# A two-block language-model forward pass on one Trainium2 core: expert down weights in 8 KB runs, shorter fillers at the router's gates, a fixed TensorE order behind them, and a reordered start

## The chip, the core and the metric

The kernel runs on one core of a Trainium2 chip. A core has five engines that each take their own instructions in order and meet through semaphores: TensorE (PE in the profile; its weight loads are listed as PEld) does matrix products into PSUM, VectorE (DVE) and ScalarE (ACT) do elementwise work and empty PSUM, GpSimd (POOL) is almost unused here, and SyncE (SP) issues nearly all transfers. Transfers run on 16 DMA engines that all queues share. The metric is the device time of one execution in microseconds (us); lower is better. All numbers are float32; products of activations with weights are made from high and low halves in a rounded type (fp32r), three products for one.

## The reference, cut to what matters

The input is 256 tokens and 16 meta tokens of width 1024. A first block has two layers, each a mixer (a short convolution, then latent attention) and a mixture of 64 experts; a second block of two layers follows, which the change leaves alone. The experts take most of the time and all of the weight traffic that the change touches.

```python
def hier_moe(hn, w_grp, w_exp, w_gate, w_up, w_down):
    g_logits = xf @ w_grp                     # 8 groups
    grp = argmax(g_logits); p_g = max(softmax(g_logits))
    e_in = (xf @ w_exp).reshape(n, 8, 8)[grp] # the 8 experts of that group
    top_p, top_i = top_k(softmax(e_in), 2)
    gate = p_g * top_p / sum(top_p)
    ...                                       # tokens sorted by expert
    def expert_block(xb, e):
        hh = silu(xb @ w_gate[e]) * (xb @ w_up[e])   # 1024 -> 256
        return hh @ w_down[e]                        # 256 -> 1024
    ...                                       # added back, weighted by gate

h = h + short_conv_mixer(rmsnorm(h), w_in, conv_w, w_out)   # layer 0
h = h + hier_moe(rmsnorm(h), ...)                           # layer 0
h = h + mla_mixer(rmsnorm(h), ...)                          # layer 1
h = h + hier_moe(rmsnorm(h), ...)                           # layer 1
return second_block(rmsnorm(h))                             # two more layers
```

## The kernel before

One Python program records all instructions, and a scheduler then sets the order on each engine. Inside `in_order(engine)` the instructions of that engine are chained as they are written; with `after=True` the chain is also tied to the last instruction before it. Elsewhere the scheduler may put one instruction between others.

**Weights.** `make_plan` (L161) lists every weight transfer of 1 MB in the order of use; SP issues them. `ahead` keeps `depth` of them under way, and 20 buffers (`WBUFS`) hold them with other tiles; a transfer waits until its buffer is free. `wload` (L119) puts row k*128+p of a matrix on partition p; `wload_flat` (L126) gives each partition one run of memory. For each expert, gate and up (1024 x 256) go by `wload_flat`: partition p gets 8 rows, 8 KB in one run. Down (256 x 1024) goes by `wload`: partition p gets rows p and 128+p, two runs of 4 KB.

**Start.** `start` (L438) issues constants and the tokens (three tiles `x` of 16, 128 and 128 rows) on SP and a few vectors on ACT's queue. The router's table `rt` (w_grp in runs of 32 bytes, w_exp in runs of 256 bytes) is written in `router` (L592, L593) on ACT's queue, and the scheduler put it early. `enter_tokens` (L507) runs ten unread products of a zero tile, turns the vectors, and transposes the tokens in eight column tiles k of three transposes each. For each k, ACT makes the high half `hnh`, DVE the low half `hn`, and ACT or DVE in turn copies the raw tile to `hT`. Then `split` makes high and low halves `wh` (ACT) and `wl` (DVE, in two pieces) of each convolution weight, and `dense` multiplies.

**Gates.** `router` sums the squares of each token by products with a column of ones; DVE copies them to `ssum` (L636). `choose` (L679) takes, on DVE, the best group, the best two experts and their one-hot rows `asg`. On TensorE it writes `keep_busy` (L673), transposes of the identity that nobody reads (48 in layer 0, 40 in layer 1), then products that count `asg` into places, then 24 more unread transposes. DVE makes `cm` from the counts and the selection `sel` from `cm`; the three low halves `hp` of the last token columns stand before `cm` on DVE. `weigh` (L734) then makes the weights of the chosen experts.

**Experts.** 16 quads of four experts each. `enter` (L842) gathers the tokens of the first two quads with `sel` (products `pa`), ACT scales them to `xg`, and the first gate products `pg` follow in four steps; the first quad's gate weights come in four transfers, each holding 2 of the 8 columns k for all four experts. `slots4` (L963) turns `sel` for one quad (`pt`), which ACT copies to `selT`. `gate_up`, then `down` (L873): two transposes of `sg`, products `pd` with the down weights, and products `pc` that add the rows back.

Of the kernel before, what the change touches and what calls it, by code (L numbers as in the profile page):

```python
# [20 lines left out]
D = 1024  # L21
KT = 8
S = 256
META = 16
T = META + S
# [3 lines left out]
CAP = 32  # L29
# [81 lines left out]
class Builder:  # L111
# [49 lines left out]
    def make_plan(self):  # L161
        a, P = self.a, []
# [8 lines left out]
        def moe(layer, following):  # L171
            for q in range(NE // 4):
# [12 lines left out]
                for e in range(4 * q, 4 * q + 4):  # L185
                    s = a["w_down"][layer, e]
                    P.append(lambda s=s: self.wload(s, 2, D))

# [22 lines left out]
        for l in range(2):  # L211
# [8 lines left out]
            for half in range(2):  # L220
                for g in range(4):
                    s = a["w_out_2"][l, 1024 * half:1024 * half + 1024]
# [284 lines left out]
    def enter_tokens(self, vectors):  # L507
# [5 lines left out]
        with self.in_order(nc.tensor):  # L513
            p = self.bank("tp")
            for i in range(10):
                self.mm(p[:, 128 * (i % 4):128 * (i % 4) + 128], zero[:, :128], zero[:, :128], True, True)
            vectors()
            for k in range(KT):
                p = self.bank()
                for (t0, n), x in zip(TILES, self.xs):  # L520
                    nc.tensor.transpose(p[:, t0:t0 + n], x[:, 128 * k:128 * k + 128], self.ident[:n, :n])
                col = g[:, k:k + 1]
                nc.scalar.activation(out=hi[:, k], in_=p[:, :T], func=AF.Identity, scale=col)
                V.scalar_tensor_tensor(lo[:, k], p[:, :T], col, hi[:, k].bitcast(F32), op0=ALU.mult, op1=ALU.subtract)
                self.copy(self.hT[:, k], p[:, :T], "va"[k % 2])
        return hi, lo
# [54 lines left out]
    def router(self, layer, new, lgt, tpt):  # L581
# [9 lines left out]
        rt = self.cp.tile([128, KT, 72], F32, name="rt", tag="rt")  # L591
        nc.scalar.dma_start(out=rt[:, :, 0:8], in_=a["w_grp"][layer].rearrange("(k p) e -> p k e", p=128))  # L592
        nc.scalar.dma_start(out=rt[:, :, 8:72], in_=a["w_exp"][layer].rearrange("(k p) e -> p k e", p=128))  # L593
        with self.in_order(V, after=True):
# [40 lines left out]
        for i, (t0, n) in enumerate(self.tiles):  # L635
            V.tensor_copy(self.ssum[:n, i:i + 1], ps[:n, i:i + 1])  # L636
        yield
# [41 lines left out]
    def choose(self, mp, tl):  # L679
# [36 lines left out]
        V.tensor_add(asg, oh2[:, :, 0], oh2[:, :, 1])  # L716
        self.keep_busy(48 - 8 * self.layer)
        pc = self.bank()
# [11 lines left out]
        self.cm = cm  # L730
        self.keep_busy(24)
        return oh2, asg, cm, L, gm, em, self.select(mp, 0)
# [140 lines left out]
    def down(self, mp, sg, selT, gcol, take, nE, by_expert=False):  # L873
# [4 lines left out]
        for c in range(2):  # L878
            nc.tensor.transpose(pt[:, M * c:M * c + M], sg[:M, 128 * c:128 * c + 128], self.ident[:M, :M])
        st = mp.tile([128, 2, 128], F32, name="st", tag="st", bufs=2)  # L880
# [6 lines left out]
        for h, c, e in order:  # L887
            self.mm(pd[h][CAP * e:CAP * e + CAP], st[:, c, CAP * e:CAP * e + CAP], ws[e][:, c, 512 * h:512 * h + 512],
                    c == 0, c == 1)
# [11 lines left out]
    def moe(self, layer):  # L901
# [5 lines left out]
        with tc.tile_pool(name="mo", bufs=1) as mp:  # L907
            NQ = NE // 4
            four = lambda: [self.take() for _ in range(4)]
            with ExitStack() as st:  # L910
                with tc.tile_pool(name="rt", bufs=1) as rp:
# [4 lines left out]
                    self.depth = DEPTH["experts"]  # L916
                    with self.in_order(nc.tensor, after=True):
                        xg, pg = self.enter(sel, four)
                    with self.in_order(V, after=True):
                        code, counts = weigh()  # L920
                mq = st.enter_context(tc.tile_pool(name="me", bufs=1))
                with self.in_order(nc.scalar, V, after=True):
                    to = self.slots4(mq, sel, 0)
                for q in range(NQ):
                    last = q == NQ - 1
# [52 lines left out]
    def overflown(self, mp, layer, code, over):  # L978
# [6 lines left out]
        with tc.If(n > 0), tc.For_i(0, n, 1) as it:  # L985
# [13 lines left out]
            gu = lambda: [self.wload_flat(a[next(names)][layer, ds(e, 1)].rearrange("o (p k) m -> p (o k m)", p=128))]  # L999
            dn = lambda: [self.wload(a["w_down"][layer, ds(e, 1)].rearrange("o f d -> (o f) d"), 2, D)]  # L1000

# [811 lines left out]
```

## Time and profile before

| | |
|---|---|
| time, median of 3 runs | 1880.17 us (1880.01 to 1880.68) |
| profiled execution, its own time | 1876.76 us |
| span of the profiled execution, first to last instruction | 1874.5 us |
| TensorE busy | 1630.6 us (87%) |
| DVE / ACT busy | 899.4 us (48%) / 622.7 us (33%) |
| HBM read | 523.20 MB, 280 GB/s over the span |
| chain that ended last, by engine | PE 53%, DMA 37%, DVE 5%, ACT 3% |
| of it, DMA into `w` from w_up / w_down / w_gate | 17% / 13% / 7% |
| of it, unread transposes (L677) | 1% |

The share of busy time is a mean over stages with different limits, so the stages are read one by one: from the chain of waits in order of time which resource ends last, from the tables by stretch how busy the transfers are and at which clock TensorE runs (1.00 is 2.4 GHz, 0.50 is 1.2 GHz), and from the timeline which instruction an engine stood waiting for (in square brackets behind a row: idle time and what ended it). The convolution fills the first 132 us, the gates and experts of layer 0 run to about 620 us, latent attention to 742 us, the gates and experts of layer 1 to about 1220 us, and the second block the rest.

### The profile page before, as it was taken

How to read it: one execution, taken by the hardware profiler on the slowest of the kernel's cores; microseconds unless marked ns; L12 is line 12 of the kernel's file. 1: busy time of each engine (PE TensorE's matmuls, PEld its weight loads, DVE VectorE, ACT ScalarE, POOL GpSimd, SP SyncE). 2: the span in 40 equal slices, each digit the busy share in tenths (PEclk: the TensorE clock that was granted, in tenths of full speed). 3: DMA queues.
4: the chain of work that ended last, by engine and by line, in shares of the span. 5: the costliest groups of instructions: out<-in, count | busy, mean ns of one | idle time of the engine just before them, and what ended most of it. 6: DMA issues, size and time to landing. Idle time of an engine off the chain costs nothing.

```text
span 1874.5 us, 32357 instructions
## 1 busy us (share of the span) xinstructions
PE 1630.6 (87%) x13515; PEld 1226.6 (65%) x13515; DVE 899.4 (48%) x2065; ACT 622.7 (33%) x1194; POOL 1.2 (0%) x6
## 2 busy tenths in 40 slices
PE   8999878787877999877767777799999999999997
PEld 7986444443443778543433333389999998999997
DVE  6753322211213675231221222288786647888673
ACT  5422011100120552210110011065456747545673
POOL 0000000000000000000000000000000000000000
PEclk8999989889988999999989898999999999999999
DMA  9667999999999337799999999944373425337340
GB/s 305 198 253 312 415 418 415 418 415 418 416 408 397 121 135 292 315 416 418 416 417 416 416 417 408 404 154 135 114 224 113 135 90 163 113 114 224 113 136 23
DMA packets 192095, 526.39 MB, mean 281 GB/s; under 512 B 15927, under 2 KB 115642, under 8 KB 160202
## 3 DMA queue, kind: packets, MB, share of 16 engines
q1 hardware_dynamic: 187644, 523.65, 73.5%
q8 instruction: 108, 1.77, 0.4%
q10 hardware_dynamic: 4302, 0.63, 0.2%
q14 instruction: 41, 0.34, 0.1%
HBM read 523.20 MB, written 1.05 MB: 280 GB/s over the span
## 4 chain that ended last, share of the span: by engine, by line
PE 53%; DMA 37%; DVE 5%; ACT 3%; issue 1%; SPq 0%; DVEq 0%; ACTq 0%
PE mm L244 30%; DMA w<-in_w_up_dram 17%; DMA w<-in_w_down_dram 13%; DMA w<-in_w_gate_dram 7%; PE A L244 5%; PE pg L244 4%; PE O L244 3%; PE pa L244 3%; PE pd L244 3%; PE pc L244 1%; PE idle L677 1%; DVE hT L505 1%; DVE wl L273 1%; PE T L244 1%; PE pt L244 1%
## 5 line engine op out<-in xcount | busy, mean ns | idle before, releaser
L244 PE MATMUL pg<-w,xg 128*32 128x256 f32 x4096 | 354.2, 433 | 116.2 <-DMA w<-in_w_gate_dram 85.0
L244 PEld LDWEIGHTS pg<-w,xg 128*32 128x32 f32 x4096 | 154.7, 123 | 278.2 <-DMA w<-in_w_gate_dram 118.4
L273 DVE TENSOR_TENSOR wl<-w,wh 128x1024 fp32r<-128x1024 f32 x192 | 231.1, 1218 | 37.9 <-ACT wh L258 29.2
L505 DVE TENSOR_TENSOR hT<-hT,pc 128x272 f32<-128x272 f32 (+1 forms) x256 | 99.7, 426 | 287.3 <-PE pc L244 287.0
L244 PE MATMUL mm<-xnh,wh 128*128 128x256 f32 x768 | 223.0, 291 | 2.7 <-ACT xnh L258 1.4
L244 PE MATMUL mm<-xnh,wl 128*128 128x256 f32 x768 | 218.0, 284 | 4.3 <-DVE wl L273 4.3
L244 PE MATMUL mm<-xn,wh 128*128 128x256 f32 x768 | 219.4, 286 | 1.8 <-DVE xn L1318 1.0
L244 PE MATMUL pd<-w,st 128*32 128x512 f32 x1024 | 183.7, 612 | 23.9 <-DVE st L239 15.5
L258 ACT ACTIVATE wh<-w 128x2048 fp32r<-128x2048 f32 x96 | 182.5, 1907 | 38.6 <-PE mm L244 24.0
L244 PEld LDWEIGHTS mm<-xnh,wl 128*128 128x128 f32 x768 | 147.6, 192 | 5.4 <-DVE wl L273 4.9
L244 PEld LDWEIGHTS mm<-xnh,wh 128*128 128x128 f32 x768 | 147.4, 192 | 5.4 <-ACT xnh L258 1.9
L244 PEld LDWEIGHTS mm<-xn,wh 128*128 128x128 f32 x768 | 147.6, 192 | 4.1 <-DVE xn L1318 1.4
L237 ACT ACTIVATE selT<-pt 128x272 fp32r<-128x272 f32 (+1 forms) x32 | 12.5, 391 | 408.9 <-PE pt L244 270.4
L894 DVE SCALAR_TENSOR_TENSOR o<-pd,gcol,o 128x512 fp32r<-128x512 f32 x64 | 48.1, 751 | 205.2 <-ACT o L893 196.9
L244 PEld LDWEIGHTS pd<-w,st 128*32 128x32 f32 x1024 | 48.0, 111 | 123.3 <-issue 75.9
L244 PE MATMUL pc<-selT,o 128*128 128x272 f32 (+1 forms) x512 | 106.8, 329 | 22.9 <-DVE hT L505 21.9
L244 PEld LDWEIGHTS pc<-selT,o 128*128 128x128 f32 x512 | 76.2, 198 | 70.3 <-issue 36.8
L893 ACT ACTIVATE o<-pd,gcol 128x512 fp32r<-128x512 f32 x64 | 44.0, 687 | 221.7 <-PE pd L244 172.7
L244 PE MATMUL pa<-sel,hp 128*128 128x256 f32 x640 | 83.6, 287 | 0.2
L244 PEld LDWEIGHTS pa<-sel,hp 128*128 128x128 f32 x640 | 78.4, 190 | 5.4 <-ACT xg L237 2.9
L870 DVE TENSOR_TENSOR sg<-sg,pg 128x256 f32<-128x256 f32 x32 | 13.5, 421 | 99.5 <-ACT sg L869 99.5
L244 PE MATMUL mm<-hnh,wh 128*128 128x272 f32 x192 | 57.1, 298 | 0.1
(531 smaller groups left out, 2867.3 us busy)
## 6 DMA issues: line engine op xcount, KB each, us to landing
w<-in_w_gate_dram SPq DMA_DIRECT2D x128, 1024.0 KB, 19.2
w<-in_w_up_dram SPq DMA_DIRECT2D x128, 1024.0 KB, 19.9
w<-in_w_down_dram SPq DMA_DIRECT2D x128, 1024.0 KB, 20.1
w<-in_w_in_dram SPq DMA_DIRECT2D x60, 1024.0 KB, 5.3
w<-in_w_out_dram SPq DMA_DIRECT2D x16, 1024.0 KB, 5.0
w<-in_conv_w_in_dram SPq DMA_DIRECT2D x12, 1024.0 KB, 13.0
w<-in_conv_w_out_dram SPq DMA_DIRECT2D x4, 1024.0 KB, 5.3
w<-in_w_o_dram SPq DMA_DIRECT2D x4, 1024.0 KB, 5.4
```

The source lines that it names most:

```text
L237: self.nc.scalar.activation(out=out, in_=in_, func=f, scale=scale)
L244: self.nc.tensor.matmul(out, lhsT, rhs, start=start, stop=stop)
L258: nc.scalar.activation(out=hi, in_=x, func=AF.Copy)
L273: V.tensor_tensor(out=lo[:, k], in0=x[:, k], in1=h[:, k], op=ALU.subtract)
L505: self.nc.vector.tensor_add(self.hT[:, k, t0:], self.hT[:, k, t0:], ps)
L677: self.nc.tensor.transpose(p[:, 128 * (i % 4):128 * (i % 4) + 128], self.ident, self.ident)
L870: nc.vector.tensor_tensor(out=sg[:M], in0=sg[:M], in1=pg[:M, 256:], op=ALU.mult)
L893: nc.scalar.activation(out=oh[:M, d], in_=pd[h][:M], func=AF.Identity, scale=gcol[:M])
L894: nc.vector.scalar_tensor_tensor(ol[:M, d], pd[h][:M], gcol[:M], oh[:M, d].bitcast(F32), op0=ALU.mult, op1=ALU.subtract)
```

## The change

Six edits.

1. Down weights go by `wload_flat`: partition p gets rows 2p and 2p+1, one run of 8 KB. So that the products meet the right rows, `down` transposes columns c, c+2, c+4, ... of `sg` (`sg[:M, c::2]`) in place of a block of 128, and reads the weights at 1024c. The loop for overflowing experts is changed alike.
2. The unread transposes at the gates fall from 48 (layer 0) and 40 (layer 1) to 26, and from 24 to 10 behind the counts.
3. TensorE's chain at the gates stays open through `enter`, `weigh` and the first `slots4`.
4. `ssum` is copied by ACT, no longer by DVE.
5. Layer 0's table `rt` is issued on SP. Layer 1's stays on ACT's queue.
6. `enter_tokens` runs 12 unread products in place of 10, gives each of the eight column tiles its own PSUM bank from the start, and copies to `hT` only behind the first weight's split.

```diff
-                    s = a["w_down"][layer, e]
-                    P.append(lambda s=s: self.wload(s, 2, D))
+                    s = a["w_down"][layer, e].rearrange("(p c) d -> p (c d)", p=128)
+                    P.append(lambda s=s: self.wload_flat(s))
...
-            p = self.bank("tp")
-            for i in range(10):
+            p = self.bank("lg")
+            for i in range(12):
...
-            for k in range(KT):
-                p = self.bank()
+            banks = [self.bank(t) for t in ("mm",) * 4 + ("tp",) * 2 + ("lg", "mm")]
+            for k, p in enumerate(banks):
...
-                self.copy(self.hT[:, k], p[:, :T], "va"[k % 2])
+        self.presplit(1)
+        for k, p in enumerate(banks):
+            self.copy(self.hT[:, k], p[:, :T], "va"[k % 2])
...
-        nc.scalar.dma_start(out=rt[:, :, 0:8], in_=a["w_grp"][layer].rearrange("(k p) e -> p k e", p=128))
-        nc.scalar.dma_start(out=rt[:, :, 8:72], in_=a["w_exp"][layer].rearrange("(k p) e -> p k e", p=128))
+        queue = nc.scalar if layer else nc.sync
+        queue.dma_start(out=rt[:, :, 0:8], in_=a["w_grp"][layer].rearrange("(k p) e -> p k e", p=128))
+        queue.dma_start(out=rt[:, :, 8:72], in_=a["w_exp"][layer].rearrange("(k p) e -> p k e", p=128))
...
-            V.tensor_copy(self.ssum[:n, i:i + 1], ps[:n, i:i + 1])
+            self.copy(self.ssum[:n, i:i + 1], ps[:n, i:i + 1], "a")
...
-        self.keep_busy(48 - 8 * self.layer)
+        self.keep_busy(26)
...
-        self.keep_busy(24)
+        self.keep_busy(10)
...
-            nc.tensor.transpose(pt[:, M * c:M * c + M], sg[:M, 128 * c:128 * c + 128], self.ident[:M, :M])
+            nc.tensor.transpose(pt[:, M * c:M * c + M], sg[:M, c::2], self.ident[:M, :M])
...
-                    with self.in_order(nc.tensor, after=True):
-                        xg, pg = self.enter(sel, four)
+                    turn = st.enter_context(ExitStack())
+                    turn.enter_context(self.in_order(nc.tensor, after=True))
+                    xg, pg = self.enter(sel, four)
...
                     to = self.slots4(mq, sel, 0)
+                turn.close()
```

TensorE at the gates of layer 1, before; `pa` gathers tokens, `pc` counts experts, `pt` turns the selection, `pg` is the first gate product:

```order
L677 MATMUL idle<-const_64 128x128 x24
L244 MATMUL pa<-sel,hp 128x256 x16
L244 LDWEIGHTS ones_462
L244 MATMUL pc<-asg,ones_462 128x64
L244 LDWEIGHTS ones_462
L244 MATMUL pc<-asg,ones_462 128x64
L957 MATMUL pt<-const_64,sel 128x128 x2
L244 MATMUL pt<-g_6550,sel 128x5 x2
L957 MATMUL pt<-const_64,sel 128x128 x2
L244 MATMUL pt<-g_6550,sel 128x5 x2
L244 MATMUL pg<-w,xg 32x256 x8
L244 MATMUL pa<-sel,hp 128x256 x8
```

And now, at the same place:

```order
L680 MATMUL idle<-const_64 128x128 x10
L244 MATMUL pa<-sel,hp 128x256 x16
L244 MATMUL pg<-w,xg 32x256 x8
L244 MATMUL pa<-sel,hp 128x256 x8
L244 MATMUL pg<-w,xg 32x256 x8
L244 MATMUL pa<-sel,hp 128x256 x8
L244 MATMUL pg<-w,xg 32x256 x16
L244 LDWEIGHTS ones_464
L244 MATMUL pc<-asg,ones_464 128x64
L244 LDWEIGHTS ones_464
L244 MATMUL pc<-asg,ones_464 128x64
L962 MATMUL pt<-const_64,sel 128x128 x2
```

The counting and turning products moved from between the gather and the first gate product to behind all four steps of `enter`; in layer 0 they stood there already. ACT's copies follow: the two `selT` of layer 1 stood ahead of the eight `xg` and now stand behind them.

ACT at the start, before:

```order
L396 ACT_TABLE_LOAD
L592 DMA rt<-in_w_grp_dram 128x8x8
L593 DMA rt<-in_w_exp_dram 128x8x64
L523 ACTIVATE hnh<-mm,vec_67 128x272 x6
L237 ACTIVATE hT<-mm 128x272
L258 ACTIVATE wh<-w 128x2048
L237 ACTIVATE hT<-mm 128x272
L523 ACTIVATE hnh<-mm,vec_67 128x272
L237 ACTIVATE hT<-mm 128x272
L523 ACTIVATE hnh<-mm,vec_67 128x272
L258 ACTIVATE wh<-w 128x2048
```

And now:

```order
L396 ACT_TABLE_LOAD
L523 ACTIVATE hnh<-mm,vec_67 128x272 x4
L523 ACTIVATE hnh<-tp,vec_67 128x272 x2
L523 ACTIVATE hnh<-lg,vec_67 128x272
L523 ACTIVATE hnh<-mm,vec_67 128x272
L258 ACTIVATE wh<-w 128x2048
L237 ACTIVATE hT<-mm 128x272 x2
L237 ACTIVATE hT<-tp 128x272
L237 ACTIVATE hT<-mm 128x272
L258 ACTIVATE wh<-w 128x2048
```

The table's two transfers left the queue, and the first weight's high half moved from behind six `hnh` to behind all eight.

SP in the convolution, now; `raw` are small vectors of the second block:

```order
L435 DMA const_462<-in_const_dram 128x1725
L123 DMA w<-in_conv_w_in_dram 128x8x256
L474 DMA raw<-in_pre_norm_dram 16x128
L474 DMA raw<-in_post_norm_dram 16x128
L474 DMA raw<-in_hgrn_lb_logits_dram 16x128
L474 DMA raw<-in_hgrn_out_norm_dram 2x128
L474 DMA raw<-in_cmp_b_k_dram 2x128
L123 DMA w<-in_conv_w_in_dram 128x8x256 x3
L474 DMA raw<-in_cmp_b_v_dram 2x128
L595 DMA rt<-in_w_grp_dram 128x8x8
L596 DMA rt<-in_w_exp_dram 128x8x64
L123 DMA w<-in_conv_w_in_dram 128x8x256 x3
```

The table stands behind nine of the twelve `conv_w_in` transfers, far behind the tokens; three of those nine stood ahead of four or five of the small vectors and now stand behind them.

## Rows read from the trace of the kernel before

**Rows 1.** Chain of waits in order of time: start us, us, what ran.
```profile
42.23 60.72 PE mm L244 x480
...
193.26 11.67 DMA w<-in_w_down_dram
```

**Rows 2.** Engines by stretch: length, PE, PEld, DVE, ACT, POOL, clock, DMA share, GB/s.
```profile
193.00:600.00 407.00, 318.61 (x2806) 171.30 (x2804) 105.65 (x262) 48.07 (x94) 0.00 (x0) 0.91 1.02 415
797.00:1205.00 408.00, 303.22 (x2669) 151.28 (x2665) 99.77 (x248) 45.38 (x80) 0.00 (x0) 0.92 1.02 416
```

**Rows 3.** Transfers in 319:325, 864:870 (down), 330:344 (gate, up) and 17:18.
```profile
DMA packets 629, 2.43 MB, mean 406 GB/s; under 512 B 39, under 2 KB 39, under 8 KB 627
...
DMA packets 637, 2.47 MB, mean 411 GB/s; under 512 B 35, under 2 KB 35, under 8 KB 637
...
DMA packets 806, 5.88 MB, mean 420 GB/s; under 512 B 89, under 2 KB 89, under 8 KB 89
...
DMA packets 348, 0.35 MB, mean 347 GB/s; under 512 B 9, under 2 KB 348, under 8 KB 348
```

**Rows 4.** Timeline at layer 0's gates: start us, us, engine, line, operation, count.
```profile
131.10 0.28 DVE L636 COPY ssum<-tp 16x1 f32<-16x1 f32 x3 [1.23 <-PE tp L244]
...
132.18 7.07 PE L677 MATMUL idle<-const 128*128 128x128 f32 x48
...
135.97 0.36 DVE L716 TENSOR_TENSOR asg<-oh 128x192 bf16<-128x192 f32 x1
136.24 1.59 DVE L656 TENSOR_TENSOR hp<-mm,hp 16x256 fp32r<-16x256 f32 x3
...
139.76 2.82 PE L677 MATMUL idle<-const 128*128 128x128 f32 x24
...
140.41 0.96 DVE L786 TENSOR_TENSOR sel<-cm,const 128x768 fp32r<-128x768 f32 x1
...
142.69 3.09 PE L244 MATMUL pa<-sel,hp 128*128 128x256 f32 x24
...
143.38 0.20 ACT L752 ACTIVATE e<-d 128x3 f32<-128x3 f32 x1 [0.70 <-DVE d L750]
...
145.70 1.07 PE L244 MATMUL pg<-w,xg 128*32 128x256 f32 x16
```

**Rows 5.** One microsecond of layer 0's first unread transposes, columns as in rows 2.
```profile
133.00:134.00 1.00, 1.00 (x6) 1.00 (x5) 0.92 (x3) 0.77 (x4) 0.00 (x0) 0.50 1.01 419
```

**Rows 6.** Timeline at layer 1's gates.
```profile
742.71 4.53 PE L677 MATMUL idle<-const 128*128 128x128 f32 x40
...
745.67 0.29 DVE L716 TENSOR_TENSOR asg<-oh 128x128 bf16<-128x128 f32 x1
...
747.69 0.69 DVE L786 TENSOR_TENSOR sel<-cm,const 128x512 fp32r<-128x512 f32 x1
...
750.24 2.14 PE L244 MATMUL pa<-sel,hp 128*128 128x256 f32 x16
...
753.94 0.38 ACT L237 ACTIVATE selT<-pt 128x256 fp32r<-128x256 f32 x1 [3.46 <-DVE code L777]
...
756.34 1.07 PE L244 MATMUL pg<-w,xg 128*32 128x256 f32 x16 [0.84 <-ACT xg L237]
```

**Rows 7.** Five microseconds of layer 1's gates, columns as in rows 2.
```profile
750.00:755.00 5.00, 3.20 (x29) 2.99 (x28) 3.30 (x18) 0.59 (x2) 0.00 (x0) 1.00 0.00 0
```

**Rows 8.** Timeline at the start, and the landing times of the three `x` transfers.
```profile
10.89 4.64 PE L521 MATMUL mm<-const,x 128*128 128x128 f32 x16 [3.94 <-DMA x<-in_x_dram]
...
16.23 1.91 ACT L258 ACTIVATE wh<-w 128x2048 fp32r<-128x2048 f32 x1
...
31.84 1.22 DVE L273 TENSOR_TENSOR wl<-w,wh 128x1024 fp32r<-128x1024 f32 x1
...
DMA to landing us min/median/max: 2.4/4.2/7.0
```

**Rows 9.** Line 879, the transposes of `sg`: duration ns min/median/max.
```profile
L879 PE MATMUL pt<-const,sg x64: 272/300/331, 161.1 to 1210.1; 128*128 128x128 f32 x64
```

More of the change, by code (lines that the diff above doesn't have):

```diff
@@ L887, in down @@
         for h, c, e in order:
-            self.mm(pd[h][CAP * e:CAP * e + CAP], st[:, c, CAP * e:CAP * e + CAP], ws[e][:, c, 512 * h:512 * h + 512],
+            self.mm(pd[h][CAP * e:CAP * e + CAP], st[:, c, CAP * e:CAP * e + CAP], ws[e][:, 1024 * c + 512 * h:1024 * c + 512 * h + 512],
                     c == 0, c == 1)
@@ L999, in overflown @@
             gu = lambda: [self.wload_flat(a[next(names)][layer, ds(e, 1)].rearrange("o (p k) m -> p (o k m)", p=128))]
-            dn = lambda: [self.wload(a["w_down"][layer, ds(e, 1)].rearrange("o f d -> (o f) d"), 2, D)]
+            dn = lambda: [self.wload_flat(a["w_down"][layer, ds(e, 1)].rearrange("o (p c) d -> p (o c d)", p=128))]
             def weigh(out):
```

## The prediction

> **What bounds the kernel now.** I read the chain of waits first, then the tables by stretch, then the timeline where the chain changes hands. The convolution is TensorE's: from 42.23 us the chain is one unbroken piece of 480 products, so whatever moves that start moves all behind it [rows 1]. At layer 0's gates the chain runs through TensorE's queue, the unread transposes among it, and at 193.26 us it passes to the weight transfers [rows 1], which keep it: over 407 us of layer 0 and 408 us of layer 1 the DMA share is 1.02 at 415 and 416 GB/s, while TensorE is busy 319 and 303 us [rows 2]. A quad's weights are 12 transfers of 1.049 MB, 12.58 MB, or 30.3 us at 415 GB/s; 815 us are 27 quads. Between the two regimes stands a gap: for five microseconds of layer 1's gates nothing at all is transferred [rows 7], since all buffers are full until the first gate products free one. So a microsecond saved ahead of the first `pg` restarts the transfers a microsecond sooner, and the layer, bound by bytes from there, ends that much sooner.
>
> **Term A, down in 8 KB runs.** Where only the two 4 KB runs of down flow, the rate is 406 and 411 GB/s; where gate and up flow in 8 KB runs it is 420 [rows 3]. A quad's down is 4.194 MB: 10.27 us at 408.5, 9.99 at 420, so 0.28 us a quad and 7.6 us over 27 quads. TensorE covers the gain: in the stretches of rows 2 it is idle for 88 and 105 us. Ends: 0, if the rate belongs to something other than the run, and -9 with a quad more and 2 GB/s more (the four stretches differ by up to 5).
>
> The Trainium skill bears on this, in "DMA: Bandwidth & Descriptors", Specifications: line rate needs pieces of at least 512 B, with nothing said for longer ones. By that page 4 KB is already at line rate, and term A would be 0; the rows, 408 against 420, speak against it, and it is a rival below.
>
> The new transposes of `sg` read every second element. No row shows such a read; an ordinary one takes 300 ns [rows 9]. At worst it doubles: two a quad, of which only some six quads (the first two and the last of each layer) are on TensorE's chain, 3.6 us; at best nothing. I take nothing, the row being of the same shape and size, and the transfer hides it in the other quads.
>
> **Term B, gates of layer 0.** Before, DVE waited 1.23 us for the sums (from 131.10 - 1.23 = 129.87, where it had copied the last `L`) and spent 0.28 on copying them [rows 4]; that leaves DVE's chain, so `asg` is done 1.5 us sooner, at 134.8 instead of 136.33. ACT takes the three copies, some 0.2 us each by its 0.20 for the like-sized `e` [rows 4], 0.6 in place of 0.28, so TensorE's next transposes, which need those banks, start about 0.3 later, and the unread ones at 132.5. At 133 us the clock is 0.50 (1.2 GHz) [rows 5]; the 48 took 7.07 us against 2.82 for 24 at full clock [rows 4], 0.1175 each, which makes about 36 cheap ones at 0.1175 and 12 dear ones at 0.235. With as many dear ones, the 26 take 14 x 0.1175 + 12 x 0.235 = 4.5 and end at 137.0. So the filler still ends behind `asg`, but 2.2 us earlier than 132.18 + 7.07 = 139.25. From its end to that of `sel` (140.41 + 0.96 = 141.37) it was 2.1, now 139.1; DVE's three low halves (1.59 us behind `asg`, so done at 136.4) are no longer in the way. `pa` stood behind 24 transposes that ended at 139.76 + 2.82 = 142.58; ten that start 0.5 behind the 26, as they did, end at 138.7, so `pa` starts with `sel`, at 139.2 instead of 142.69. `xg` waits for ACT's `e`, which ended 2.2 us behind `sel`: 141.3, and two copies later (0.38 each, as the copy of the same 128x256 in rows 6) `pg` starts at about 142.1 against 145.70. **-3.6 us.** Ends: -2.0 with all 26 at the low clock (6.1 us), -4.8 with none (then the low halves set `cm`). The gap between filler and `pa` stays under half a microsecond.
>
> **Term C, gates of layer 1.** The clock is full there (40 in 4.53 us, 0.113 each [rows 6]). Starting 0.3 later, as in layer 0, 26 end at 743.0 + 2.95 = 745.95 instead of 742.71 + 4.53 = 747.24; `asg`, freed of the sums by the same step, comes about a microsecond before 745.96, and its two low halves (two thirds of the 1.59 in rows 4) are done by 746.0. `sel` ends near 747.3 (before: 747.69 + 0.69 = 748.38), and `pa` starts at 747.4 instead of 750.24, where the 24 held it. Then the order: TensorE ran counting and turning products behind `pa`, and ACT two `selT` ahead of `xg`; `selT` waited 3.46 us for DVE's `code` [rows 6], so the first `pg` came 6.1 us behind `pa`, at 756.34. With `pg` next, as in layer 0, it starts when `xg` lets it: `sel` + 2.2 + two copies = about 750.2. **-6.1 us.** What moved behind `enter` is paid there, in a stretch whose end the transfers set. Ends: -3.0 if the low clock meets the 26 (3 us longer), -7.6 if the moved products also find a free place.
>
> **Term D, start.** Three steps. First, the tokens: their three transfers land 2.4, 4.2 and 7.0 us after issue; the last, which TensorE waited 3.94 us for, is the slow one [rows 8]. It shares the engines with the table's runs of 32 and 256 bytes, which now go elsewhere. Between 0 and 7.0 - 4.2 = 2.8 us; I take 2.0, near the sibling transfer's time, with a little left for the weights that still flow beside it. Second, the first `wh` (1.91 us) now waits for all eight `hnh`. Sixteen transposes took 4.64 us, 0.87 a tile; eight tiles end at 10.89 + 6.96 = 17.85, the last `hnh` some 0.4 later (rows 6's copy again), `wh` at about 20.15 instead of 16.23 + 1.91 = 18.14: +2.0. Third, DVE now does a whole `wl` half (1.22 us) ahead of the first norm instead of behind ACT's part of it: +1.0. Sum 3.0 - 2.0 = **+1.0 us** for the piece that began at 42.23. Ends: +3.0 with the tokens no earlier, and -1.5 if unbroken transposes also raise the clock before the first products. Two more unread products end long before 10.89 and cost nothing. `rt` adds two issues to SP behind nine weight transfers; the later convolution weights wait for that, but the unbroken 60.72 us [rows 1] show them ahead of use, and `rt` itself is read only near its end. Without that cover one late weight costs 3.0 us (1.049 MB at 347 GB/s [rows 3]).
>
> **Sum.** -7.6 - 3.6 - 6.1 + 1.0 = -16.3 us. The profiled execution took 1876.76 us, so its like would be 1860.5; the median of the three runs is 1880.17, 3.4 above it, and from that the forecast is **1863.9 us**.
>
> **Rivals.**
> - *The run's length does nothing.* Then 408 against 420 comes from where down lies, not how it is cut: term A is 0 and the time 1871.5. For it: rows 3 show two tensors, not two cuts of one. Against: four stretches in two layers agree, and 1 KB runs at 347 GB/s continue the line.
> - *TensorE's clock falls at the gates.* Fewer unread products leave the engine less to do just where it fell to 0.50 [rows 5]. Terms B and C shrink to -2.0 and -3.0: 1880.17 - 7.6 - 2.0 - 3.0 + 1.0 = 1868.6. Against: what is left ends within half a microsecond of the next work.
> - *The tokens come no earlier* (the move of `rt` doesn't do what it should): term D is +3.0, the time 1865.9. For it: the weights, not the table, could be what slows the last token tile.
> - *Slower: down flows worse than today.* All down transfers then cost more on the resource that sets the layers' time. At the 347 GB/s of the 1 KB runs [rows 3] a quad's down takes 12.09 us, 1.82 more than now: 27 x 1.82 = 49, less the other 8.7 gained, is +40.3, or 1920.5. It decides from 0.32 us a quad (8.7 / 27), that is below 396 GB/s. Against: gate and up do the same form at 420.
>
> **How the numbers follow.** Forecast as sized 0.55 (its own range 1860 to 1868), run length 0.13, clock 0.17, tokens 0.12, slower 0.03. The range reaches from 1858 (terms A, B and C together some 6 us better) to 1873 (the first rival with a poor start); it leaves out what is worse than the first rival and the last one. A difference under 0.2% (3.8 us) can hardly be told from none. All cases but the last lie more than that below 1880.17; for two of them falling together with stride and start at their bad ends I set 0.04 on "within 0.2%", and 0.03 on slower: faster 0.93.
>
> **What the profile after should show.** Down's stretches with 128 runs a transfer and 420 GB/s; a quad every 30.0 us instead of 30.3. In layer 0, `pg` about 12.2 us behind the end of DVE's `L` copies (129.87 before) instead of 15.8, `pa` right behind `sel`. In layer 1, `pg` within 3 us of `pa` and no idle TensorE between. At the start, tokens near 8.8 us, `wh` near 18, the long piece from about 43. I am wrong if down's stretches stay at 408, if the clock reads 0.50 over the first `pa`, or if TensorE waits for `sg` transposes.

## The result and the profile after

The changed kernel takes 1860.5 us (median of 4 runs, 1857.0 to 1861.7), the kernel before beside it 1880.4; the ratio is 0.9888 with a 95% interval of 0.9874 to 0.9902, or 18 to 24 us less. The forecast was 1863.9, the range 1858 to 1873. The profiled execution took 1856.99 us with a span of 1854.9; before it was 1876.76 and 1874.5.

Five instants cut both traces into the stretches of the prediction's terms: the 145th product of the convolution (the first of the long piece), the first gate product `pg` and the last group of `pd` of each layer. In us, from the timelines:

| stretch | before | after | difference |
|---|---|---|---|
| start to the 145th product (D) | 42.16 | 39.21 | -2.95 |
| to `pg` of layer 0 (B) | 103.54 | 101.27 | -2.27 |
| to its last `pd` (A) | 459.57 | 456.00 | -3.57 |
| to `pg` of layer 1 (C) | 151.07 | 145.04 | -6.03 |
| to its last `pd` (A) | 454.52 | 449.57 | -4.95 |
| to the end | 663.64 | 663.81 | +0.17 |

In the chain of waits of the changed kernel, in order of time, the convolution runs unbroken from 17.03 us on, with only TensorE's turning of small vectors (0.20 us) between the two rows, where before it had been broken and restarted at 42.23 [rows 1]:

```profile
17.03 22.05 PE mm L244 x150
39.28 60.73 PE mm L244 x480
```

Transfers of the changed kernel in the same stretches as rows 3, the first two down (319:325 and 864:870), the third mostly gate and up (330:344):

```profile
DMA packets 343, 2.51 MB, mean 418 GB/s; under 512 B 38, under 2 KB 38, under 8 KB 38
...
DMA packets 347, 2.52 MB, mean 421 GB/s; under 512 B 39, under 2 KB 39, under 8 KB 39
...
DMA packets 811, 5.91 MB, mean 422 GB/s; under 512 B 90, under 2 KB 90, under 8 KB 90
```

The pieces of 4 KB, some hundred a microsecond before, are gone, and the three stretches run alike. The timeline at layer 0's gates (start us, us, engine, line, operation, count), to be laid beside rows 4, and one microsecond of it with the granted clock after the busy times, as in rows 5:

```profile
128.49 0.26 ACT L237 ACTIVATE ssum<-tp 16x1 f32<-16x1 f32 x3 [2.45 <-PE tp L244]
128.60 0.11 DVE L691 MEMSET cm<- 128x64 f32 x1 [1.69 <-PE tp L244]
...
130.05 5.15 PE L680 MATMUL idle<-const 128*128 128x128 f32 x26
...
133.25 0.36 DVE L719 TENSOR_TENSOR asg<-oh 128x192 bf16<-128x192 f32 x1
133.53 1.57 DVE L659 TENSOR_TENSOR hp<-mm,hp 16x256 fp32r<-16x256 f32 x3
...
135.71 1.29 PE L680 MATMUL idle<-const 128*128 128x128 f32 x10
...
136.36 0.96 DVE L789 TENSOR_TENSOR sel<-cm,const 128x768 fp32r<-128x768 f32 x1
...
137.46 3.09 PE L244 MATMUL pa<-sel,hp 128*128 128x256 f32 x24 [0.46 <-DVE ms L372]
...
139.26 0.20 ACT L755 ACTIVATE e<-d 128x3 f32<-128x3 f32 x1 [0.70 <-DVE d L753]
...
140.48 1.07 PE L244 MATMUL pg<-w,xg 128*32 128x256 f32 x16
```

```profile
131.00:132.00 1.00, 1.00 (x7) 1.00 (x6) 0.86 (x9) 0.00 (x0) 0.00 (x0) 0.50 1.03 420
```

The gather now follows `sel`, as forecast, but the 26 unread transposes took 5.15 us, not 4.5: the granted clock was 0.50 (1.2 GHz) from 127.6 to 134.4. The second row shows something that wasn't forecast: DVE no longer copies the sums, but its next instruction still waits for TensorE's products, as the copy had. Layer 1's gates, beside rows 6:

```profile
733.12 0.17 DVE L695 MAX8 gm<-L 128x8 f32<-128x8 f32 x1 [1.03 <-PE T L244]
...
733.84 3.00 PE L680 MATMUL idle<-const 128*128 128x128 f32 x26
...
736.78 0.29 DVE L719 TENSOR_TENSOR asg<-oh 128x128 bf16<-128x128 f32 x1
...
738.31 0.69 DVE L789 TENSOR_TENSOR sel<-cm,const 128x512 fp32r<-128x512 f32 x1
...
739.15 2.14 PE L244 MATMUL pa<-sel,hp 128*128 128x256 f32 x16 [0.66 <-DVE ms L372]
...
741.52 1.07 PE L244 MATMUL pg<-w,xg 128*32 128x256 f32 x16 [0.23 <-ACT xg L237]
...
747.68 0.23 PE L244 MATMUL pc<-asg,ones 128*128 128x64 bf16 x2
...
749.40 0.38 ACT L237 ACTIVATE selT<-pt 128x256 fp32r<-128x256 f32 x1 [2.64 <-DVE code L780]
```

From `pa` to `pg` it is 2.4 us in place of 6.1; counting and turning run behind `enter`. And the start, beside rows 8:

```profile
8.08 2.96 PE L521 MATMUL mm<-const,x 128*128 128x128 f32 x10 [1.53 <-DMA x<-in_x_dram]
...
14.79 1.90 ACT L258 ACTIVATE wh<-w 128x2048 fp32r<-128x2048 f32 x1
...
39.02 0.27 PE L481 MATMUL mm<-const,raw 54*128 54x54 f32 x1
```

The last row is TensorE turning 54 small vectors of the second block, just ahead of the 145th product. Before, the same instruction had stood 1.48 us idle; here it waits for nothing.

### The profile page after: what moved, and what is told of

Read it like the earlier page. It is cut to its first block, busy times and chain, and to the rows that moved or that the text cites. A ratio compares the mean times of both kernels' runs of the same rounds, so it can differ in the third digit from the quotient of the medians.

```text
span 1854.9 us, 32240 instructions
## 1 busy us (share of the span) xinstructions
PE 1623.8 (88%) x13455; PEld 1227.5 (66%) x13455; DVE 899.1 (48%) x2060; ACT 623.6 (34%) x1199; POOL 1.8 (0%) x6
## 3 DMA queue, kind: packets, MB, share of 16 engines
HBM read 523.20 MB, written 1.05 MB: 283 GB/s over the span
## 4 chain that ended last, share of the span: by engine, by line
PE 54%; DMA 37%; DVE 5%; ACT 3%; issue 1%; SPq 0%; DVEq 0%; ACTq 0%
PE mm L244 31%; DMA w<-in_w_up_dram 17%; DMA w<-in_w_down_dram 12%; DMA w<-in_w_gate_dram 8%; PE A L244 6%; PE pg L244 4%; PE O L244 3%; PE pd L244 2%; PE pa L244 2%; PE pc L244 2%; DVE hT L505 1%; PE T L244 1%; DVE wl L273 1%; PE T L1755 1%; PE pt L244 0%
## 5 line engine op out<-in xcount | busy, mean ns | idle before, releaser
L244 PE MATMUL pd<-w,st 128*32 128x512 f32 x1024 | 174.6, 604 | 21.0 <-DVE st L239 15.5
```

The costliest lines, as they stand in the source:

```text
L244: self.nc.tensor.matmul(out, lhsT, rhs, start=start, stop=stop)
```

## Experiments

The open points were whether the run's length makes term A, which edit makes B and C and what the clock does to them, and why the start gained 2.95 us where a loss of 1.0 was forecast. A difference of 2 us lies inside the spread of the times, so the smaller terms are read in the stretches of the table above. For all kernels, in us; the first two columns are instants, the next four the stretches of the table above, in its order. In kernels named "old" one edit is undone:

| kernel | tokens' transposes start | 145th product | to `pg` | to last `pd` | to `pg` 1 | to last `pd` | ratio to before, 95% |
|---|---|---|---|---|---|---|---|
| before | 10.89 | 42.16 | 103.54 | 459.57 | 151.07 | 454.52 | |
| after | 8.08 | 39.21 | 101.27 | 456.00 | 145.04 | 449.57 | 0.9888 (0.9874 to 0.9902) |
| after_again | 8.29 | 38.17 | 100.03 | 457.53 | 144.98 | 452.12 | 0.9884 (0.9864 to 0.9905) |
| down_only | 8.58 | 41.82 | 104.05 | 456.08 | 150.20 | 450.80 | 0.9949 (0.9932 to 0.9966) |
| down_4k_gap | 9.47 | 39.31 | 100.04 | 459.91 | 145.06 | 454.30 | 0.9945 (0.9926 to 0.9964) |
| down_2k | 9.96 | 41.73 | 100.04 | 461.33 | 145.08 | 455.06 | 0.9953 (0.9933 to 0.9973) |
| rt_only | 9.53 | 39.63 | 103.22 | 459.81 | 151.76 | 455.77 | 0.9988 (0.9974 to 1.0002) |
| rt_old | 9.98 | 40.91 | 100.03 | 457.10 | 145.27 | 451.53 | 0.9899 (0.9878 to 0.9919) |
| enter_only | 9.79 | 40.97 | 103.24 | 459.88 | 151.91 | 455.32 | 0.9991 (0.9976 to 1.0007) |
| vec_late | 9.59 | 39.31 | 103.62 | 459.81 | 149.25 | 454.88 | 0.9971 (0.9960 to 0.9982) |
| order_old | 8.16 | 38.56 | 101.92 | 453.74 | 150.17 | 450.14 | 0.9923 (0.9896 to 0.9950) |
| fill_old | 8.53 | 38.90 | 101.74 | 455.97 | 146.21 | 449.67 | 0.9917 (0.9891 to 0.9943) |
| ssum_old | 9.39 | 40.66 | 100.14 | 456.04 | 141.86 | 451.98 | 0.9882 (0.9847 to 0.9918) |
| no_fill | 9.55 | 40.76 | 102.36 | 456.11 | 145.26 | 449.55 | 0.9908 (0.9873 to 0.9944) |

### Term A: the length of a run

**down_only**: edit 1 of the diff, added to the kernel before.

```diff
-                    s = a["w_down"][layer, e]
-                    P.append(lambda s=s: self.wload(s, 2, D))
+                    s = a["w_down"][layer, e].rearrange("(p c) d -> p (c d)", p=128)
+                    P.append(lambda s=s: self.wload_flat(s))
...
-            nc.tensor.transpose(pt[:, M * c:M * c + M], sg[:M, 128 * c:128 * c + 128], self.ident[:M, :M])
+            nc.tensor.transpose(pt[:, M * c:M * c + M], sg[:M, c::2], self.ident[:M, :M])
...
```

> The kernel before with down weights in 8 KB runs and nothing else. Theory (the length of a run sets the rate): down's stretches rise from 406-411 to 418-422 GB/s, and each layer's stretch from the first gate product pg to the last pd (before 459.57 and 454.52 us) shortens by 3.6 to 5.0 us as in the changed kernel, together 8.5: time about 1872, with nothing else moved. Rival 1 (408 GB/s belongs to where down lies): stretches stay at 406-411 and the time at 1880. Rival 2 (part of the changed kernel's gain in the layers came from the earlier first pg, not from the runs): less than 6 us gained in the two stretches together.

Its transfers in 319:325:

```profile
DMA packets 343, 2.51 MB, mean 418 GB/s; under 512 B 38, under 2 KB 38, under 8 KB 38
```

The layers' stretches are 3.5 and 3.7 us shorter and the time 8.4 us (medians 1869.67 and 1878.07). Rival 1 falls. The first `pg` was no earlier here in layer 0 and 0.9 us earlier in layer 1, and the stretches gained 7.2 us, so rival 2 falls too. One pair of profiles doesn't give this gain to a microsecond: in the seven profiles with down in one piece (without order_old, whose layer 0 differs) the two stretches together are 4.4 to 8.5 us shorter than before, 6.9 in the mean.

**down_2k** and **down_4k_gap**: the changed kernel, with gaps in the buffer between the pieces that a partition gets, four of 2 KB or two of 4 KB. In HBM the 8 KB stay one run. The code is that of down_2k; the products read the weights at the places moved by the gaps.

```diff
+    def wload_gaps(self, src):
+        w = self.wp.tile([128, WSLOT], F32, name="w", tag="w")[:, :4 * 544]
+        self.nc.sync.dma_start(out=w.rearrange("p (x d) -> p x d", x=4)[:, :, :512],
+                               in_=src.rearrange("p (x d) -> p x d", x=4))
+        return w
...
-                    P.append(lambda s=s: self.wload_flat(s))
+                    P.append(lambda s=s: self.wload_gaps(s))
...
```

> The changed kernel with down written to the buffers in four pieces of 2 KB per partition (gaps between them), all else the same. Theory (each piece costs a fixed extra time): 8192 bytes at 420 GB/s take 19.50 ns of all engines together, 4096 at 408.5 take 10.03, so a piece costs 0.56 ns beside 2.31 ns per KB; 2 KB pieces then run at 2048/5.30 = 387 GB/s, a quad's down takes 10.84 us instead of 9.98, and 28 quads cost 24 us: about 1884.5. Rival (no cost per piece, 408 is a second level that all shorter runs down to a limit share): 408 GB/s, +8 us, 1868.5.

> The changed kernel with down written in two pieces of 4 KB with a gap between them in the buffer; a partition's 8 KB are still one run in HBM. If the length of the pieces sets the rate: 406 to 411 GB/s as in the kernel before, the layers' stretches from pg to the last pd 3.5 to 5.5 us longer than in the changed kernel (456.0 and 449.6), time about 1868.5. If the run in HBM sets it and pieces of 4 KB cost nothing: 418 to 422 GB/s, 1860.5 (the 408 of 2 KB pieces would then be the first sign of a cost per piece).

Down's stretches of down_2k (315:321), then of down_4k_gap (313:319):

```profile
DMA packets 1225, 2.44 MB, mean 406 GB/s; under 512 B 38, under 2 KB 38, under 8 KB 1224
```

```profile
DMA packets 632, 2.45 MB, mean 408 GB/s; under 512 B 39, under 2 KB 39, under 8 KB 630
```

Two pieces of 4 KB out of one run of 8 KB cost what the kernel before paid: 408 GB/s, stretches of 459.9 and 454.3, and 8.2 us of time against the changed kernel's 1860.5 (9.9 against after_again's 1858.7, taken beside it). So neither the run in HBM nor where down lies makes the rate, but the piece that is written. The packets are cut with it (632 in place of 343 in six microseconds); whether the gap in the buffer or the shorter packet counts was not tried. The theory of a fixed cost per piece falls: it asked for 387 GB/s at 2 KB and 24 us, and found 406 and 8.7. From 2 to 4 KB almost nothing changes (406 to 408), to 8 KB there is a step.

### Terms B and C: the gates

**fill_old**, **no_fill**, **ssum_old**, **order_old**: the changed kernel with one edit undone, or (no_fill) without any unread transposes.

First fill_old; in no_fill both calls are left out.

```diff
-        self.keep_busy(26)
+        self.keep_busy(48 - 8 * self.layer)
...
-        self.keep_busy(10)
+        self.keep_busy(24)
```

> The changed kernel with the old counts of unread transposes, 48 and 40, then 24. Theory (they stand in TensorE's queue ahead of the counts and of the gather): pg of layer 0 comes 2.2 to 3.6 us later against the start of the long piece (101.2 us in the changed kernel), pg of layer 1 2.8 us later against the last pd of layer 0 (145.0): time 1865.5 to 1867. Rival (the shorter ones let the clock fall over the gather, which gives most of it back): under 2 us in both layers together, 1861 to 1862.5.

From the end of the last sums of layer 1 to `pg` it takes 10.43 us instead of 8.50, and in layer 0 101.74 from the 145th product instead of the 100.03 of after_again, in both of which the clock stood at 1.00 there: 1.7 and 1.9 us, 3.6 together, against 5.0 to 6.4 expected. The theory holds in kind, and the size is 57 to 73% of it. The time, 1863.4, lies between the two expectations.

> The changed kernel without any unread transposes at the gates. Theory 1 (they only stand in the queue): pg of layer 0 comes 0.7 us sooner, since cm then waits for DVE's low halves alone, layer 1 unchanged: 1859.8. Theory 2 (they hold the clock): the granted clock reads 0.50 over the gather pa in both layers; 24 and 16 products at twice 0.129 us cost 3.1 and 2.1 us, and the products behind them as much again until the clock rises: 4.5 to 8 us, 1865 to 1868.5.

The gather of layer 0 and of layer 1 in no_fill, and a microsecond of the first:

```profile
137.74 5.46 PE L244 MATMUL pa<-sel,hp 128*128 128x256 f32 x24 [1.96 <-DVE ms L372]
...
741.06 3.50 PE L244 MATMUL pa<-sel,hp 128*128 128x256 f32 x16 [1.68 <-DVE ms L372]
```

```profile
138.00:139.00 1.00, 1.00 (x6) 1.00 (x6) 0.64 (x5) 0.22 (x1) 0.00 (x0) 0.50 0.00 0
```

TensorE stood idle ahead of the gather and then ran it at 0.50: 5.46 us for what takes 3.09, and 3.50 for 2.14. `pg` comes 2.3 us later than in after_again in layer 0 and 1.0 later in layer 1 (9.52 from the last sums), 3.3 together. Theory 2 is right in kind and high in size (4.5 to 8 us); the time (1861.8) can't be told from that of the changed kernel.

The edit of ssum_old:

```diff
-            self.copy(self.ssum[:n, i:i + 1], ps[:n, i:i + 1], "a")
+            V.tensor_copy(self.ssum[:n, i:i + 1], ps[:n, i:i + 1])
```

> The changed kernel with the sums of squares copied by DVE again. Theory: in layer 0 DVE's chain to asg starts about 1.1 us later, of which some 0.7 are hidden by the unread transposes, so pg comes 0.4 to 0.8 later; in layer 1, where TensorE already waits for asg, pg comes 1.0 later: together 1.5, time 1862. Rival (hidden in both layers): no difference in either trace.

Layer 1 takes 9.20 us from the end of the last sums to `pg` instead of 8.50, but that isn't the copies: in this profile the clock was 0.50 over the unread transposes (730.7 to 734.1 us). In order_old, with ACT's copies, it was so at the same place. The two profiles, ssum_old first:

```profile
730.37 4.67 PE L680 MATMUL idle<-const 128*128 128x128 f32 x26
...
736.52 2.13 PE L244 MATMUL pa<-sel,hp 128*128 128x256 f32 x16
```

```profile
730.44 4.67 PE L680 MATMUL idle<-const 128*128 128x128 f32 x26
```

From the end of the last sums to `pa` it is 7.02 us here and 6.96 in order_old. In layer 0 it is 100.14 to `pg`, against 100.04 in down_2k, whose spell of half clock (3.4 us) is as long and as far ahead of `pg`. And `asg` ends 5.3 and 4.1 us behind the last sums here, 5.2 and 4.0 in after_again. So the copies are worth 0.1 us a layer, as the waits of DVE behind them have stayed; the rival comes nearest. What ties DVE's next instruction to the sums wasn't tried. Nothing shows in the time. This profile has 3 us less in the latent attention and as much more in the second block; why is open.

The edit of order_old:

```diff
-                    turn = st.enter_context(ExitStack())
-                    turn.enter_context(self.in_order(nc.tensor, after=True))
-                    xg, pg = self.enter(sel, four)
+                    with self.in_order(nc.tensor, after=True):
+                        xg, pg = self.enter(sel, four)
...
-                turn.close()
```

> The changed kernel without the order fixed past the gates: counting and turning products of layer 1 stand again between the gather pa and the first gate product pg. Theory: from pa to pg it takes 6.1 us again instead of 2.4, the transfers restart that much later, and layer 1 ends 3.7 us later: time 1864.2. Rival (the moved products are paid back behind pg, so that the transfers' end moves less): under 2 us, 1860.5 to 1862.5. Layer 0 the same in both.

The timeline of order_old at layer 1's gates:

```profile
736.59 2.13 PE L244 MATMUL pa<-sel,hp 128*128 128x256 f32 x16
...
738.55 0.23 PE L244 MATMUL pc<-asg,ones 128*128 128x64 bf16 x2
...
741.44 0.39 ACT L237 ACTIVATE selT<-pt 128x256 fp32r<-128x256 f32 x1 [3.08 <-DVE code L780]
...
744.39 1.93 PE L244 MATMUL pg<-w,xg 128*32 128x256 f32 x16 [0.84 <-ACT xg L237]
```

The old wait for `code` is back, and from `pa` to `pg` it is 7.8 us; the clock fell to 0.50 in the stall, hence more than 6.1. It isn't paid back in layer 1: from layer 0's last `pd` to layer 1's it takes 600.3 us, against 594.6, 596.8 and 597.1 in the changed kernel, rt_old and after_again. But in layer 0, where without this edit the scheduler now also puts the turning ahead of `pg` (the kernel before had it behind), `pg` is later and the stretch behind it 2.3 us shorter, and layer 0's last `pd` comes 1.6 us sooner than in the changed kernel, counted from the 145th product; "layer 0 the same" was wrong. The time, 1862.5 and 2.0 us above the changed kernel's, stands at the upper end of the rival, while layer 1 alone lost 3.2 to 5.7 us, with the half clock's share in it, against the theory's 3.7.

**after_again**: the changed kernel, unaltered.

> The changed kernel once more. Theory (a half-clock spell falls on the gates in one execution and not in another): another place or length of the spell than 127.5 to 133.5 us, so that from the long piece to layer 0's pg it takes 100.0 us or, with no spell, under 100, instead of 101.2; time 1860.5. Rival (the spell belongs to the order of work): again about 5 to 6 us of 0.50 from four microseconds ahead of the unread transposes on, 101.2 us.

Its unread transposes in layer 0, and a microsecond of them:

```profile
128.07 3.00 PE L680 MATMUL idle<-const 128*128 128x128 f32 x26
```

```profile
130.00:131.00 1.00, 1.00 (x10) 0.83 (x9) 0.90 (x9) 0.00 (x0) 0.00 (x0) 1.00 0.99 403
```

No half clock, 3.00 us for the 26, and `pg` 100.03 us behind the 145th product, which rt_old and down_4k_gap confirm with 100.03 and 100.04. So 1.2 us of the 101.27 was the spell, nearly 7 us long, and the rival falls. A spell half as long costs nothing at `pg`: down_2k had 0.50 from 130.9 to 134.3 us and 100.04.

### Term D: the start

**rt_only** and **enter_only**: edit 5 or edit 6 of the diff alone, added to the kernel before; **rt_old**: the changed kernel without edit 5.

```diff
-        nc.scalar.dma_start(out=rt[:, :, 0:8], in_=a["w_grp"][layer].rearrange("(k p) e -> p k e", p=128))
...
+        queue = nc.scalar if layer else nc.sync
+        queue.dma_start(out=rt[:, :, 0:8], in_=a["w_grp"][layer].rearrange("(k p) e -> p k e", p=128))
...
-            for i in range(10):
+            for i in range(12):
...
+            banks = [self.bank(t) for t in ("mm",) * 4 + ("tp",) * 2 + ("lg", "mm")]
...
-                self.copy(self.hT[:, k], p[:, :T], "va"[k % 2])
+        self.presplit(1)
+        for k, p in enumerate(banks):
+            self.copy(self.hT[:, k], p[:, :T], "va"[k % 2])
```

The first three lines are of edit 5, the rest of edit 6.

> The kernel before with layer 0's router table issued on SP behind the small vectors. Theory: the last token tile lands about 2.8 us sooner (TensorE's transposes start at 8.1 instead of 10.89), the first dense product at about 15.4 instead of 18.19, and the long unbroken piece of TensorE at 39.5 to 42.2 (39.5 if its start hangs on the chain from the tokens; 42.2 if it hangs on the small vectors and those come no earlier); time 1877.5 to 1880. Rival (the weights, not the table, slow the tokens): transposes still start at 10.9 and the time is 1880.

> The changed kernel with layer 0's router table back on ACT's queue. The prediction's step: the tokens come 2.0 us later, transposes start near 10.5, time 1862.5. Theory now (their landing differs from run to run, 8.1 to 10.9, whichever queue has the table): transposes start anywhere between 8 and 11 and the time is that of the changed kernel, 1860.5.

> The kernel before with the reordered entry of the tokens and nothing else. The prediction's steps: tokens at 10.89, first high half of a weight 2.0 us later, a whole low half ahead of the first norm, long piece 3.0 us later (45.2), time 1883. Theory after the result: the first dense product comes about 1.6 us later (19.8), but the small vectors, which this edit moves ahead of three weight transfers on SP, are there when TensorE turns them, so the 1.48 us that it waited there go: long piece at about 42.1, time 1880.

The tokens' transposes start at 10.89, 8.58, 9.98, 9.79 and 9.59 us with the table on ACT's queue (mean 9.8), and between 8.08 and 9.96 in the nine profiles with it on SP (mean 9.0). The means differ by 0.8 us, and the ranges overlap so far that it may be nothing; the 2.0 had come from the landing times of one profile, and neither time shows a gain. From the transposes' start to the first `wh` it is 5.0 to 5.3 us in the four profiles without edit 6 and 5.4 to 6.7 in the ten with it (6.2 in the mean): +0.9 where +2.0 was forecast.

**vec_late**: the kernel before, with the small vectors loaded at the same place but turned a quarter of the convolution later.

```diff
                 if g == 1:
-                    self.start_more()
+                    turn = self.load_more()
+                if g == 2:
+                    self.start_more(turn)
```

> The kernel before with the small vectors of the second block loaded at the same place on SP but turned on TensorE a quarter of the convolution later. Theory (TensorE's wait ahead of the long piece is for their transfers): from the start of the first weight's high half to the 145th product of the convolution it takes 24.5 to 24.8 us, as where no such wait is seen, instead of 26.0 (before) and 28.3 (down alone); time 1876.5 to 1879. Rival (the chain of waits is right and it is ACT's high half behind yh): 26 us or more, TensorE still idle there, 1880.

From the first `wh` to the 145th product it takes 24.4 us (14.93 to 39.31), against 25.9 before and 28.3 in down_only, and the chain of vec_late shows one piece up to the moved instruction:

```profile
16.89 40.74 PE mm L244 x294
57.63 0.20 PE mm L481
```

In down_only the wait at that instruction has its true name:

```profile
41.57 0.32 PE L481 MATMUL mm<-const,raw 54*128 54x54 f32 x1 [4.32 <-DMA raw<-in_hgrn_lb_logits_dram]
```

The wait was for the small vectors, and the rival (ACT's `wh` behind `yh`, the name in the chain of before) falls. The wait's length differs between executions: 1.48 us before, 4.32 in down_only, 0.1 in rt_only, three kernels with the same order of these vectors. With edit 6 it is nothing in eight of ten profiles, but 0.49 and 0.47 us in order_old and fill_old, where the profile names ACT's `yh`:

```profile
38.39 0.23 PE L481 MATMUL mm<-const,raw 54*128 54x54 f32 x1 [0.49 <-ACT yh L258]
```

There the last small vector (`cmp_b_v`), which still stands behind three weight transfers, landed at 38.20 and 38.53 us, 0.2 us ahead of the instruction. The time gained is 5.1 us by the medians (1874.62 and 1879.71), more than the 0.7 to 3.2 expected; the trace gives 2.85 to the start, of which 1.3 are earlier tokens, and the rest to stretches that the edit doesn't touch.

## Why the prediction was right, and where it was not

**Term A, right.** -7.6 forecast, -8.5 in the two stretches of the first pair (before and after), -7.2 in down_only's, -6.9 in the mean of seven profiles; so the 8.5 has a microsecond or so of chance in it. The rate of 420 that was read from gate and up is what down got (418 to 421). By the Trainium skill, "DMA: Bandwidth & Descriptors", Specifications (line rate from 512 B on), the term would have been 0 and down_only at 1878; it measured 1869.7, so here the measurement differs from the page. The stride in the read of `sg` costs 36 ns a transpose by the medians, far from the doubling that bounded it (line 882 of the changed kernel, beside rows 9):

```profile
L882 PE MATMUL pt<-const,sg x64: 281/336/389, 155.9 to 1190.3; 128*128 128x128 f32 x64
```

**Term B, right in size, one step wrong; -3.6 forecast.** `pg` is 2.3 us sooner in the first pair; against profiles of the changed gates without the long spell of half clock, 3.5. `pa` starts with `sel` as written. The step that failed is `asg`, which was to come 1.5 us sooner once the sums had left DVE: the copies left, DVE's wait for the sums did not, and `asg` gained 0.1 (ssum_old). That it did no harm is partly luck. With the spell, the unread transposes ended behind `asg` as forecast; but DVE's low halves, said to be out of the way, then stood directly ahead of `cm`, and `sel` came out where the other path had put it: in down_2k, whose spell (3.4 us) is as long as that of before, `sel` ends 8.0 us behind the last sums, and the forecast's 139.1 is 8.0 behind them too. The low end, -4.8 with no spell, rested on the early `asg` and wasn't reached: after_again has none, and 3.5.

What the shorter filler bought depends on the clock. From the end of the last sums to `pg` it is 11.1 us with 26 transposes in after_again and down_2k, without a spell and with one of 3.4 us; with 48 it is 13.0 in down_only and 12.9 in fill_old without one, and 14.2 to 14.6 with one of 3.4 us in the other four. So 1.7 to 1.8 us is its worth at full clock, and the rest is a low-clock spell that the old filler didn't hide.

The sentence that a microsecond ahead of `pg` is a microsecond at the layer's end is too simple: from the 145th product to layer 0's last `pd` the profiles after_again (557.56) and after (557.27) end alike although their `pg` differ by 1.2. Of the gain at `pg`, about 2 to 2.3 us reach the end (-5.55 and -5.84 in all, of which term A is some 3.5). What binds the first quads then, TensorE or a transfer, was not tried.

**Term C, right in size, by two errors that cancel.** -6.1 forecast, -6.0 measured. From the last sums to `pa` it is 2.3 us less where 2.8 was forecast, since here too `asg` gained 0.1 instead of about 1; and from `pa` to `pg` 3.7 less (6.1 to 2.4) where the prediction's numbers give 3.3. The filler makes the first part (2.2 us at `pa`, 1.9 at `pg` in fill_old), the order the second, the sums at most 0.1.

**Term D, wrong in size and sign: +1.0 forecast, -2.95 measured.** Three steps failed. The tokens' -2.0 took one profile's landing for a property of the kernel; it varies by more than that. The +1.0 for a whole `wl` half ahead of the norm counted on the chain through the norm, `yh` and `wh` up to 42.23 [rows 1]; the norm's first `ms` did come 0.9 us later behind the first `wh` (16.2 us instead of 15.3), but no product waited for it. And the wait that did hold TensorE, 1.48 us for the small vectors, was not seen, because the chain named ACT's `wh`, the last that had ended. Edit 6 removed it but for half a microsecond in two profiles: with it three weight transfers stand behind five of those vectors on SP instead of ahead of them, and enter_only has no wait there. With the tokens 2.8 us earlier in this pair and `wh` 1.4 later against them, -1.4 and -1.5 make the -2.95; the 2.8 is one execution's luck, as above.

The sum came out 3.4 us below the forecast, which is nearly term D's error (4.0), with B 1.3 short and A 0.9 over. That holds for this pair; with after_again in place of after the spans differ by 17.3 us and not by 19.6, so part of the agreement, as of the error, is chance. Of the rivals, the run's length and slower fell with down_only, the tokens' happened in part (no gain from the table, but no loss either), and the clock's showed up in one of two profiles of the changed kernel, for 1.2 us at `pg`. Its counter-argument, half a microsecond between the filler and the next work, was too small (TensorE stands idle 1.2 us ahead of the counts and 1.05 ahead of `pa` in after_again), yet the clock stayed at 1.00 there.

## What to carry to other kernels

Where transfers set the time, compare the rates of stretches whose pieces differ in size, and test with a re-cut of the same tensor; here 8 KB in one piece was 3% better than two of 4 KB, and it was worth more than any other edit. A name in the chain of waits that follows an engine's end by a fraction of a microsecond may hide a transfer: look which data the waiting instruction reads, and when they were issued. Taking an instruction off an engine doesn't take off the wait ahead of it: look what the next instruction waits for. Before a landing time or a low-clock spell becomes a term of a sum, or a reading of an experiment, look at it in more than one profile.

## What the runs showed of the hardware

The rate by piece written was 347 GB/s at 1 KB (weights of the convolution, in HBM too in runs of 1 KB), 406 at 2 KB, 408 at 4 KB and 420 at 8 KB: no line of a constant cost per piece, but a step between 4 and 8 KB that one run in HBM doesn't remove.

At layer 0's gates the spell of 0.50 belongs to the execution more than to the kernel: with 26 unread transposes the same kernel had nearly 7 us of it in one profile and none in another. Over all kernels it stood there in three of seven profiles with 26 and in four of six with 48. With none of them it lasted from about 129.7 to 143 us, over the whole gather. So the fillers are worth about 3 us at the two gates, and halving them cost nothing that the runs show.

At layer 1's first `pg` it follows the order of work. In all six profiles where counting and turning stand ahead of `pg`, the clock fell to 0.50 between 3.5 us ahead of `pg` and 1.2 behind it, for 3.4 to 6.9 us; in none of the seven with the new order and fillers did it fall there. The second gather `pa` behind `pg`, before and after:

```profile
757.34 2.07 PE L244 MATMUL pa<-sel,hp 128*128 128x256 f32 x8
```

```profile
742.52 1.21 PE L244 MATMUL pa<-sel,hp 128*128 128x256 f32 x8
```

The prediction had read 1.00 up to 755 us [rows 7] and left this out. What it costs at the layer's end was not tried.
